# A matmul with a subtraction on one core: own semaphores, a PE loop over six m tiles, and shared weight loads

## The chip, the cores and the metric

The kernel runs on one core of a Trainium2 chip. The metric is the device time of one execution in microseconds; lower is better. The engines are named as the profile names them: PE is TensorE's matmul, PEld its weight loads, DVE is VectorE, ACT is ScalarE, SP issues the transfers. All 16 DMA engines of the core serve it.

## The reference

```python
batch, m, k, n = 16, 512, 1024, 768
def reference(x, weight, sub_value):          # all float32
    return (np.matmul(x, weight) - sub_value).astype(np.float32)
```

With the batch flattened there are 64 m tiles of 128 rows. 61.9 MB are read from memory and 25.2 MB written.

## The kernel before

For each m tile, ACT casts x to f16, the cast tile is transposed, PE multiplies it with the f16 weights that stay on chip (16 matmuls of 384 columns), and DVE subtracts. Most tiles are transposed by PE (four transposes of 32-bit words, put between the matmuls of the tile two before) and copied out by ACT. Fourteen tiles, in seven pairs at 18, 24, ... 54, are transposed by DVE instead, in sixteen instructions for each pair. The parts that matter here:

```python
LEAD_DVE = 7                 # a pair's casts are issued seven tiles ahead
PER = 4                      # DVE transposes issued behind one subtraction
ON_DVE = frozenset(range(18, 60, 6))
...
x16p_pool = ctx.enter_context(tc.tile_pool(name="x16p_pool", bufs=2))   # a pair, cast
xtp_pool = ctx.enter_context(tc.tile_pool(name="xtp_pool", bufs=2))     # a pair, transposed
psum_o_pool = ctx.enter_context(tc.tile_pool(name="psum_o", bufs=3, space=bass.MemoryType.PSUM))
...
def matmuls(mi, c):          # each matmul loads its own weights
    ...
    for r in range(2):
        for h in range(2):
            keep(nc.tensor.matmul(po_t[mi][:, h, :NS], xt_t[mi][:, 2*P*c + r : 2*P*(c+1) : 2],
                                  w_sb[:, c, r, h*NS : (h+1)*NS], ...))
...
for mi in range(HEAD, n_mt):
    t = mi + TA              # TA = 2
    tr = transposes(t) if t < n_mt and t - t % 2 not in ON_DVE else []
    for c in range(n_c):
        matmuls(mi, c)
        if tr:
            tr[c]()          # the fourth is followed by ACT's copy
    for t in range(mi, n_mt):
        if t - lead(t) == mi:    # LEAD_DVE for a pair's tiles, 4 for others
            cast(t)
    finish(mi)               # DVE: subtract, then the transfer out if a group is done
    if mi + LEAD_DVE - 1 in ON_DVE:
        waiting += transposes_dve(mi + LEAD_DVE - 1)
    for f in waiting[:PER]:
        f()
    del waiting[:PER]
```

A framework puts in the semaphores and hands out the buffers; everything is written out in a straight line.

## Time and profile before

| | before |
|---|---|
| time, median of 3 | 211.0 us (210.91 to 211.28) |
| span in the profile | 209.4 us |
| DMA engines busy | 97.7%, mean 417 GB/s |
| granted clock of PE, mean (1 is full speed) | 0.998 |

A share of busy time does not say who waits for whom. The views to read are the stretches (busy time of each engine in a given piece of the span) and the timeline. "T" below means the moment at which one tile's matmuls end and the next tile's begin. The lines are in the prediction.

### The profile page before, as it was taken

How to read it: one execution, taken by the hardware profiler on the slowest of the kernel's cores; microseconds unless marked ns; L12 is line 12 of the kernel's file. 1: busy time of each engine (PE TensorE's matmuls, PEld its weight loads, DVE VectorE, ACT ScalarE, POOL GpSimd, SP SyncE). 2: the span in 40 equal slices, each digit the busy share in tenths (PEclk: the TensorE clock that was granted, in tenths of full speed). 3: DMA queues.
4: the chain of work that ended last, by engine and by line, in shares of the span. 5: the costliest groups of instructions: out<-in, count | busy, mean ns of one | idle time of the engine just before them, and what ended most of it. 6: DMA issues, size and time to landing. Idle time of an engine off the chain costs nothing.

```text
span 209.4 us, 2967 instructions
## 1 busy us (share of the span) xinstructions
PE 198.4 (95%) x1249; PEld 130.4 (62%) x1249; DVE 114.1 (54%) x186; ACT 112.6 (54%) x115; POOL 0.7 (0%) x6
## 2 busy tenths in 40 slices
PE   7998789999979999999999999999999999999990
PEld 2464467676656576676666666667666766766660
DVE  0342044206149849929946965992994795332231
ACT  3555565675396183655727629355573760765410
POOL 1000000000000000000000000000000000000000
PEclk9999999999999999999999999999999999999999
DMA  6999999999999999999999999999999999999994
GB/s 221 420 426 424 424 438 439 433 443 426 391 455 415 442 427 423 454 413 432 435 421 449 423 413 444 451 418 421 418 441 440 423 437 418 426 446 427 415 383 167
DMA packets 5629, 87.22 MB, mean 417 GB/s; under 512 B 624, under 2 KB 624, under 8 KB 2032
## 3 DMA queue, kind: packets, MB, share of 16 engines
q1 hardware_dynamic: 5616, 87.03, 97.7%
q8 instruction: 10, 0.16, 0.3%
q14 instruction: 3, 0.02, 0.0%
HBM read 61.87 MB, written 25.17 MB: 416 GB/s over the span
## 4 chain that ended last, share of the span: by engine, by line
PE 68%; DMA 20%; ACT 4%; DVE 3%; SPq 1%; issue 1%
PE psum_o L177 60%; DMA x_ring<-in_x_dram 20%; PE psum_t L144 8%; ACT x_tile L135 2%; DVE xtp_tile L165 2%; ACT xt_tile L151 1%; DVE so_ring L189 1%; SPq L110 1%; SPq L122 1%; ACT x16p_tile L132 0%
## 5 line engine op out<-in xcount | busy, mean ns | idle before, releaser
L177 PE MATMUL psum_o<-w_sb,xt_tile 128*128 128x384 f16 x800 | 145.7, 326 | 1.7 <-ACT xt_tile L151 1.1
L177 PEld LDWEIGHTS <-xt_tile 128*128 128x128 f16 x800 | 78.2, 98 | 41.5 <-ACT xt_tile L151 1.9
L189 DVE TENSOR_TENSOR so_ring<-psum_o,so_ring 128x768 f32<-128x768 f32 x64 | 60.7, 957 | 61.2 <-PE psum_o L177 41.1
L151 ACT COPY xt_tile<-psum_t 128x1024 f16<-128x1024 f16 x50 | 50.6, 1012 | 75.7 <-PE psum_t L144 74.9
L165 DVE STREAM_TRANSPOSE xtp_tile<-x16p_tile 32x256 f32<-32x256 f32 x112 | 48.8, 436 | 18.9 <-ACT x16p_tile L132 17.2
L144 PE MATMUL psum_t<-ident,x_tile 128*128 128x128 f32 x200 | 52.5, 275 | 2.8 <-ACT x_tile L135 2.4
L135 ACT CAST x_tile<-x_ring 128x1024 f16<-128x1024 f32 x50 | 51.6, 1049 | 5.5 <-DMA x_ring<-in_x_dram 5.5
L177 PE MATMUL psum_o<-w_sb,xtp_tile 128*128 128x384 f16 x224 | 42.9, 326 | 0.3 <-DVE xtp_tile L165 0.3
L144 PEld LDWEIGHTS psum_t<-ident,x_tile 128*128 128x128 f32 x200 | 27.8, 142 | 16.8 <-ACT x_tile L135 4.7
L177 PEld LDWEIGHTS <-xtp_tile 128*128 128x128 f16 x224 | 21.8, 98 | 10.4 <-DVE xtp_tile L165 0.7
L132 ACT CAST x16p_tile<-x_ring 128x1024 f16<-128x1024 f32 x14 | 14.6, 1046 | 5.8 <-DMA x_ring<-in_x_dram 4.7
L205 PE MATMUL psum_o<-idle_x,idle_w 128*128 128x512 f16 x25 | 8.8, 508 | 1.3 <-DVE idle_x L200 1.3
L112 DVE CAST w_sb<-so_ring 128x768 f16<-128x768 f32 x8 | 4.1, 556 | 10.5 <-DMA so_ring<-in_weight_dram 10.5
L205 PEld LDWEIGHTS <-idle_w 128*128 128x128 f16 x25 | 3.0, 120 | 5.0 <-issue 3.2
L135 ACT ACT_TABLE_LOAD x1 | 1.3, 1283 | 0.7 <-PEq L277 0.7
L199 DVE MEMSET idle_w<- 128x64 uint32 x1 | 0.1, 112 | 0.8 <-PEq L277 0.8
masks.py:199 POOL TENSOR_SCALAR_AFFINE_SELECT ident<-ident 128x128 f32<-128x128 f32 x1 | 0.3, 292 | 0.1
L200 DVE MEMSET idle_x<- 128x256 uint32 x1 | 0.3, 272 | 0.0
masks.py:197 POOL MEMSET ident<- 128x128 f32 x1 | 0.2, 205 | 0.3 <-POOLq L277 0.3
L277 POOL MEMSET const-bfloat16-1.0<- 128x1 bf16 x1 | 0.1, 101 | 0.0
L277 POOL MEMSET const-uint8-127<- 128x1 uint8 x1 | 0.1, 101 | 0.0
L277 POOL MEMSET const-float32-0.0<- 128x1 f32 x1 | 0.1, 98 | 0.2 <-issue 0.2
(1 smaller groups left out, 0.1 us busy)
## 6 DMA issues: line engine op xcount, KB each, us to landing
so_ring<-in_sub_value_dram SPq DMA_DIRECT2D x7, 3072.0 KB, 24.2
out_dram<-so_ring SPq DMA_DIRECT2D x7, 3072.0 KB, 31.2
x_ring<-in_x_dram SPq DMA_DIRECT2D x5, 4096.0 KB, 22.3
x_ring<-in_x_dram SPq DMA_DIRECT2D x2, 2560.0 KB, 23.3
x_ring<-in_x_dram SPq DMA_DIRECT2D x3, 1536.0 KB, 19.8
so_ring<-in_weight_dram SPq DMA_DIRECT2D x4, 768.0 KB, 8.7
x_ring<-in_x_dram SPq DMA_DIRECT2D x3, 512.0 KB, 6.2
so_ring<-in_sub_value_dram SPq DMA_DIRECT2D x1, 1536.0 KB, 22.2
```

Source lines behind the costliest of these rows:

```text
L110: keep(nc.sync.dma_start(out=st, in_=w_c[at]))
L112: keep(nc.vector.tensor_copy(out=w_sb[:, at, r], in_=st[:, r]))
L122: keep(nc.sync.dma_start(out=here, in_=there))
L132: keep(nc.scalar.copy(out=x16_t["pair", first][:, mi - first], in_=x_in))
L135: keep(nc.scalar.copy(out=x16_t[mi], in_=x_in))
L144: keep(nc.tensor.transpose(ps_t[mi].bitcast(F32)[:, c * P : (c + 1) * P], x16_t[mi].bitcast(F32)[:, c * P : (c + 1) * P], ident,))
L151: keep(nc.scalar.copy(out=xt_t[mi], in_=ps_t.pop(mi)))
L165: keep(nc.vector.transpose(xt[b * Q : (b + 1) * Q, :, a * Q : (a + 1) * Q], x16[a * Q : (a + 1) * Q, :, b * Q : (b + 1) * Q],))
L177: keep(nc.tensor.matmul(po_t[mi][:, h, :NS], xt_t[mi][:, 2 * P * c + r : 2 * P * (c + 1) : 2], w_sb[:, c, r, h * NS : (h + 1) * NS], start ...
L189: keep(nc.vector.tensor_tensor(out=o, in0=po_t.pop(mi)[:, :, :NS], in1=o, op=mybir.AluOpType.subtract))
L205: keep(nc.tensor.matmul(idle_o[:, 0], idle_w, idle_x, start=True, stop=True))
L277: nc = _bacc.Bacc("TRN2", target_bir_lowering=False, num_devices=1)
```

## The change

The intent is a short PE program: six m tiles as the body of a loop that runs seven times. Waits in the loop compare semaphores with registers that only grow, so the kernel makes its own semaphores in one critical section and names its own buffers. Two matmuls that use the same stationary operand share one load. What goes with it, because the body of six tiles must name the same buffers each time: one output buffer for a DVE pair, a shorter lead, and six transposes at a time. The core of the diff:

```diff
+N16, NXT, NPT, NPO = 4, 4, 2, 3
+N16P, NXTP = 2, 1
-LEAD_DVE = 7
-PER = 4
+LEAD_DVE = 5
+PER = 6
+LOOP = (15, 6, 7)
...
+        with self.engine.Fori(0, len(bodies)):
+            self.emit(first, value=lambda sem, v: regs[sem.name], after=after)   # after: reg_add
...
         for r in range(2):
+            weights = xt[:, 2 * P * c + r : 2 * P * (c + 1) : 2]
+            pe.add(lambda weights=weights: nc.tensor.ldweights(weights, tile_position=(0, 0)), ...)
             for h in range(2):
-                keep(nc.tensor.matmul(
+                pe.add(lambda r=r, h=h, weights=weights: loaded_matmul(
...
+        first, size, times = LOOP
+        pe.emit(pe.ops[: marks[first]])
+        pe.emit_loop([pe.ops[a:b] for a, b in zip(ends, ends[1:])])
+        pe.emit(pe.ops[ends[-1] :])
```

More of the change, by code (lines that the diff above doesn't have):

```diff
@@ L31, with __init__, add, emit @@
 ]
+class Queue:
+    def __init__(self, nc, engine):
+        self.nc, self.engine, self.ops, self.seen = nc, engine, [], {}
+    def add(self, make, waits=(), then=None, always=False):
+        need = []
+        for sem, value in waits:
+            if value > 0 and (always or self.seen.get(sem.name, 0) < value):
+                self.seen[sem.name] = value
+                need.append((sem, value))
+        self.ops.append((make, need, then))
+    def emit(self, ops, value=lambda sem, v: v, after=lambda sem: None):
+        for make, need, then in ops:
+            for sem, v in need[:-1]:
+                self.engine.wait_ge(sem, value(sem, v))
+                after(sem)
+            ins = make()
+            if need:
+                sem, v = need[-1]
+                ins.wait_op(sem, value(sem, v), "sem-ge")
+                after(sem)
+            if then:
+                ins.then_inc(*then)
+    def emit_loop(self, bodies):
+        first, second = bodies[0], bodies[1]
+        sems, firsts, steps = {}, {}, {}
+        for one in bodies:
+            assert [[s.name for s, _ in n] for _, n, _ in one] == [[s.name for s, _ in n] for _, n, _ in first]
+        for make, need, then in first:
+            for sem, v in need:
+                sems[sem.name] = sem
+                firsts.setdefault(sem.name, []).append(v)
+        later = {}
+        for make, need, then in second:
+            for sem, v in need:
+                later.setdefault(sem.name, []).append(v)
+        grow = {s: later[s][0] - firsts[s][0] for s in firsts}
+        for n, one in enumerate(bodies):
+            at = {s: iter(v) for s, v in firsts.items()}
+            for _, need, _ in one:
+                for sem, v in need:
+                    assert v == next(at[sem.name]) + n * grow[sem.name]
+        for s, v in firsts.items():
+            steps[s] = [b - a for a, b in zip(v, v[1:] + [v[0] + grow[s]])]
+        regs = {s: self.engine.alloc_register(f"at_{s}") for s in sems}
+        for s, r in regs.items():
+            self.engine.reg_mov(r, firsts[s][0])
+        left = {s: iter(v) for s, v in steps.items()}
+        def after(sem):
+            step = next(left[sem.name])
+            if step:
+                self.engine.reg_add(regs[sem.name], regs[sem.name], step)
+        with self.engine.Fori(0, len(bodies)):
+            self.emit(first, value=lambda sem, v: regs[sem.name], after=after)
@@ L43 @@
     nc = tc.nc
-    keep = tc.keep_in_program_order
     x_flat = x.flatten_outer_dims()
@@ L60 @@
     w_c = weight.rearrange("(c p r) n -> c p r n", p=P, r=2)
-    def rows(view, mi, n):
-        return view[mi // S][:, mi % S : mi % S + n]
-    const_pool = ctx.enter_context(tc.tile_pool(name="const", bufs=1))
-    w_pool = ctx.enter_context(tc.tile_pool(name="w_pool", bufs=1))
-    x_pool = ctx.enter_context(tc.tile_pool(name="x_pool", bufs=1))
-    x16_pool = ctx.enter_context(tc.tile_pool(name="x16_pool", bufs=CA + 2))
-    xt_pool = ctx.enter_context(tc.tile_pool(name="xt_pool", bufs=TA + 3))
@@ L70 @@
-    x16p_pool = ctx.enter_context(tc.tile_pool(name="x16p_pool", bufs=2))
-    xtp_pool = ctx.enter_context(tc.tile_pool(name="xtp_pool", bufs=2))
-    so_pool = ctx.enter_context(tc.tile_pool(name="so_pool", bufs=1))
-    psum_t_pool = ctx.enter_context(tc.tile_pool(name="psum_t", bufs=2, space=bass.MemoryType.PSUM))
-    psum_o_pool = ctx.enter_context(tc.tile_pool(name="psum_o", bufs=3, space=bass.MemoryType.PSUM))
-    ident = const_pool.tile([P, P], F32)
-    make_identity(nc, ident)
-    w_sb = w_pool.tile([P, n_c, 2, N], F16)
@@ L82, with sbuf, psum @@
-    x_ring = x_pool.tile([P, NX, K], F32)
-    so_ring = so_pool.tile([P, NSO, N], F32)
-    x16_t, xt_t, ps_t, po_t = {}, {}, {}, {}
+    ctx.enter_context(tc.tile_critical(no_gpsimd_drain=True))
+    def sbuf(name, shape, dtype):
+        return ctx.enter_context(nc.sbuf_tensor(name, shape, dtype)).ap()
+    def psum(name, shape, dtype):
+        return ctx.enter_context(nc.psum_tensor(name, shape, dtype)).ap()
+    ident = sbuf("ident", [P, P], F32)
+    w_sb = sbuf("w_sb", [P, n_c, 2, N], F16)
@@ new lines @@
+    x_ring = sbuf("x_ring", [P, NX, K], F32)
+    so_ring = sbuf("so_ring", [P, NSO, N], F32)
+    x16_b = sbuf("x16_b", [P, N16, K], F16)
+    xt_b = sbuf("xt_b", [P, NXT, K], F16)
+    x16p_b = sbuf("x16p_b", [P, N16P, 2, K], F16)
+    xtp_b = sbuf("xtp_b", [P, NXTP, 2, K], F16)
+    idle_w = sbuf("idle_w", [P, P], F16)
+    idle_x = sbuf("idle_x", [P, 512], F16)
+    pt_b = psum("pt_b", [P, NPT, K], F16)
+    po_b = psum("po_b", [P, NPO, 2, 512], F32)
+    counter = {}
+    for name in ("ident", "idle", "w", "cast", "evac", "pair", "turn", "mul", "finish"):
+        counter[name] = tc.alloc_semaphore(name)
@@ new lines, with count @@
+    so_far = dict.fromkeys(counter, 0)
+    def count(name):
+        so_far[name] += 1
+        return (counter[name], 1)
+    sp, pe = Queue(nc, nc.sync), Queue(nc, nc.tensor)
+    act, dve, pool = Queue(nc, nc.scalar), Queue(nc, nc.vector), Queue(nc, nc.gpsimd)
+    pool.add(lambda: nc.gpsimd.memset(ident, 0.0), then=count("ident"))
+    pool.add(lambda: nc.gpsimd.affine_select(
+        out=ident, in_=ident, compare_op=mybir.AluOpType.not_equal, fill=1.0, base=0,
+        pattern=[[-1, P]], channel_multiplier=1,
+    ), waits=[(counter["ident"], 1)], then=count("ident"))
@@ new lines, with loaded_matmul @@
+    ready = (counter["pair"], counter["evac"])
+    def loaded_matmul(out, weights, moving, start, stop):
+        with nc.discard():
+            full = nc.tensor.matmul(out, weights, moving, start=start, stop=stop).ins
+        return nc.tensor.add_instruction(mybir.InstMatmult(
+            name=nc.get_next_instruction_name(), engine=full.engine, ins=list(full.ins), outs=list(full.outs),
+            start_tensor_calc=full.start_tensor_calc, stop_tensor_calc=full.stop_tensor_calc,
+            tile_size=full.tile_size, tile_position=full.tile_position, ldweights=False,
+        ))
@@ L88, with take @@
+    landed = {}
+    cast_at, evac_at, pair_at, turn_at, mul_at, finish_at, w_at = {}, {}, {}, {}, {}, {}, {}
+    slot = {}
+    used = dict.fromkeys(("x16", "xt", "x16p", "xtp", "pt", "po"), 0)
+    holder = {}
+    def take(pool_name, n, mi):
+        b = used[pool_name] % n
+        used[pool_name] += 1
+        slot[pool_name, mi] = b
+        before = holder.get((pool_name, b))
+        holder[pool_name, b] = mi
+        return b, before
     todo = list(TRANSFERS)
     done = {"w": set(), "x": set(), "s": set(), "o": set(), "cast": set(), "finish": set()}
+    staged = {}
@@ L105, in issue @@
             done[kind] |= span
+            sem = tc.alloc_semaphore(f"{kind}{at}")
             if kind == "w":
@@ L109, in issue @@
                 st = so_ring[:, first : first + 2]
-                keep(nc.sync.dma_start(out=st, in_=w_c[at]))
+                sp.add(lambda st=st, at=at: nc.sync.dma_start(out=st, in_=w_c[at]), then=(sem, 16))
                 for r in range(2):
-                    keep(nc.vector.tensor_copy(out=w_sb[:, at, r], in_=st[:, r]))
+                    dve.add(
+                        lambda at=at, r=r, st=st: nc.vector.tensor_copy(out=w_sb[:, at, r], in_=st[:, r]),
+                        waits=[(sem, 16)], then=count("w"),
+                    )
+                    staged[first + r] = so_far["w"]
+                w_at[at] = so_far["w"]
                 continue
@@ L118, in issue @@
             there = view[at // S][:, at % S : at % S + n]
-            if kind == "o":
-                keep(nc.sync.dma_start(out=there, in_=here))
-            else:
-                keep(nc.sync.dma_start(out=here, in_=there))
+            waits = []
+            if kind == "x" and need:
+                waits.append((counter["cast"], max(cast_at[t] for t in need)))
+            if kind == "s":
+                for t in need:
+                    waits.append((landed["o", t], 16))
+                for t in span:
+                    if t % NSO in staged:
+                        waits.append((counter["w"], staged.pop(t % NSO)))
+            if kind == "o":
+                waits.append((counter["finish"], max(finish_at[t] for t in need)))
+            for t in span:
+                landed[kind, t] = sem
+            if kind == "o":
+                here, there = there, here
+            sp.add(lambda here=here, there=there: nc.sync.dma_start(out=here, in_=there), waits, (sem, 16))
     def cast(mi):
@@ L128, in cast @@
         first = mi - mi % 2
+        waits = [(landed["x", mi], 16)]
         if first in ON_DVE:
             if mi == first:
-                x16_t["pair", mi] = x16p_pool.tile([P, 2, K], F16, name="x16p_tile")
-            keep(nc.scalar.copy(out=x16_t["pair", first][:, mi - first], in_=x_in))
-        else:
-            x16_t[mi] = x16_pool.tile([P, K], F16, name="x16_tile")
-            keep(nc.scalar.copy(out=x16_t[mi], in_=x_in))
+                b, before = take("x16p", N16P, mi)
+                if before is not None:
+                    waits.append((counter["pair"], pair_at[before]))
+            to = x16p_b[:, slot["x16p", first], mi - first]
+        else:
+            b, before = take("x16", N16, mi)
+            if before is not None:
+                waits.append((counter["turn"], turn_at[before]))
+            to = x16_b[:, b]
+        act.add(lambda: nc.scalar.copy(out=to, in_=x_in), waits, count("cast"))
+        cast_at[mi] = so_far["cast"]
         issue()
@@ L141, in f @@
             def f():
+                waits = []
                 if c == 0:
-                    ps_t[mi] = psum_t_pool.tile([P, K], F16, name="psum_t")
-                keep(nc.tensor.transpose(
-                    ps_t[mi].bitcast(F32)[:, c * P : (c + 1) * P],
-                    x16_t[mi].bitcast(F32)[:, c * P : (c + 1) * P],
-                    ident,
-                ))
-                if c == n_c - 1:
-                    xt_t[mi] = xt_pool.tile([P, K], F16, name="xt_tile")
-                    keep(nc.scalar.copy(out=xt_t[mi], in_=ps_t.pop(mi)))
-                    x16_t.pop(mi)
+                    b, before = take("pt", NPT, mi)
+                    waits.append((counter["cast"], cast_at[mi]))
+                    if before is not None:
+                        waits.append((counter["evac"], evac_at[before]))
+                b = slot["pt", mi]
+                words = pt_b[:, b].bitcast(F32)[:, c * P : (c + 1) * P]
+                from_ = x16_b[:, slot["x16", mi]].bitcast(F32)[:, c * P : (c + 1) * P]
+                last = c == n_c - 1
+                pe.add(lambda: nc.tensor.transpose(words, from_, ident), waits, count("turn") if last else None)
+                if last:
+                    turn_at[mi] = so_far["turn"]
+                    d, before = take("xt", NXT, mi)
+                    waits = [(counter["turn"], turn_at[mi])]
+                    if before is not None:
+                        waits.append((counter["mul"], mul_at[before]))
+                    act.add(lambda: nc.scalar.copy(out=xt_b[:, d], in_=pt_b[:, b]), waits, count("evac"))
+                    evac_at[mi] = so_far["evac"]
             return f
@@ L156, in transposes_dve @@
     def transposes_dve(mi):
-        x16 = x16_t.pop(("pair", mi)).bitcast(F32).rearrange("p j (c q) -> p (j c) q", c=n_c)
-        xt_p = xtp_pool.tile([P, 2, K], F16, name="xtp_tile")
-        xt_t[mi], xt_t[mi + 1] = xt_p[:, 0], xt_p[:, 1]
-        xt = xt_p.bitcast(F32).rearrange("p j (c m) -> p (j c) m", c=n_c)
-        def one(a, b):
-            def f():
-                keep(nc.vector.transpose(
+        x16 = x16p_b[:, slot["x16p", mi]].bitcast(F32).rearrange("p j (c q) -> p (j c) q", c=n_c)
@@ new lines, in transposes_dve, with one @@
+        blocks = [(a, b) for a in range(P // Q) for b in range(P // Q)]
+        def one(n, a, b):
+            def f():
+                waits = []
+                if n == 0:
+                    d, before = take("xtp", NXTP, mi)
+                    waits.append((counter["cast"], cast_at[mi + 1]))
+                    if before is not None:
+                        waits.append((counter["mul"], mul_at[before + 1]))
+                xt = xtp_b[:, slot["xtp", mi]].bitcast(F32).rearrange("p j (c m) -> p (j c) m", c=n_c)
+                last = n == len(blocks) - 1
+                dve.add(lambda: nc.vector.transpose(
@@ L166, in f @@
                     xt[b * Q : (b + 1) * Q, :, a * Q : (a + 1) * Q],
                     x16[a * Q : (a + 1) * Q, :, b * Q : (b + 1) * Q],
-                ))
+                ), waits, count("pair") if last else None)
+                if last:
+                    pair_at[mi] = so_far["pair"]
             return f
-        return [one(a, b) for a in range(P // Q) for b in range(P // Q)]
+        return [one(n, a, b) for n, (a, b) in enumerate(blocks)]
     def matmuls(mi, c):
+        first = mi - mi % 2
@@ L173, in matmuls @@
+        on_dve = first in ON_DVE
+        waits = []
         if c == 0:
-            po_t[mi] = psum_o_pool.tile([P, 2, 512], F32, name="psum_o")
+            b, before = take("po", NPO, mi)
+            waits.append((counter["pair"], pair_at[first]) if on_dve else (counter["evac"], evac_at[mi]))
+            if before is not None:
+                waits.append((counter["finish"], finish_at[before]))
+        if mi <= HEAD:
+            waits.append((counter["w"], w_at[c]))
+        xt = xtp_b[:, slot["xtp", first], mi - first] if on_dve else xt_b[:, slot["xt", mi]]
@@ L175, in matmuls @@
+        po = po_b[:, slot["po", mi]]
         for r in range(2):
+            weights = xt[:, 2 * P * c + r : 2 * P * (c + 1) : 2]
+            pe.add(lambda weights=weights: nc.tensor.ldweights(weights, tile_position=(0, 0)), [w for w in waits if w[0] in ready])
+            waits = [w for w in waits if w[0] not in ready]
             for h in range(2):
-                keep(nc.tensor.matmul(
-                    po_t[mi][:, h, :NS],
-                    xt_t[mi][:, 2 * P * c + r : 2 * P * (c + 1) : 2],
+                last = c == n_c - 1 and r == 1 and h == 1
+                pe.add(lambda r=r, h=h, weights=weights: loaded_matmul(
+                    po[:, h, :NS],
+                    weights,
@@ L182, in matmuls @@
                     stop=(c == n_c - 1 and r == 1),
-                ))
+                ), waits, count("mul") if last else None)
+                waits = []
+        if c == n_c - 1:
+            mul_at[mi] = so_far["mul"]
     def finish(mi):
@@ L188, in finish @@
         o = so_ring[:, mi % NSO].rearrange("p (h n) -> p h n", h=2)
-        keep(nc.vector.tensor_tensor(
-            out=o, in0=po_t.pop(mi)[:, :, :NS], in1=o, op=mybir.AluOpType.subtract
-        ))
+        po = po_b[:, slot["po", mi]]
+        dve.add(lambda: nc.vector.tensor_tensor(
+            out=o, in0=po[:, :, :NS], in1=o, op=mybir.AluOpType.subtract
+        ), [(landed["s", mi], 16), (counter["mul"], mul_at[mi])], count("finish"))
+        finish_at[mi] = so_far["finish"]
         issue()
     issue()
-    idle_w = const_pool.tile([P, P], F16)
-    idle_x = const_pool.tile([P, 512], F16)
-    nc.vector.memset(idle_w, 0.0)
-    nc.vector.memset(idle_x, 0.0)
-    idle_o = psum_o_pool.tile([P, 2, 512], F32, name="psum_o")
+    starts = len(dve.ops)
+    dve.add(lambda: nc.vector.memset(idle_w, 0.0), then=count("idle"))
+    dve.add(lambda: nc.vector.memset(idle_x, 0.0), then=count("idle"))
+    dve.ops = dve.ops[starts:] + dve.ops[:starts]
     def idle(n):
         for _ in range(n):
-            keep(nc.tensor.matmul(idle_o[:, 0], idle_w, idle_x, start=True, stop=True))
+            pe.add(
+                lambda: nc.tensor.matmul(po_b[:, NPO - 1, 0], idle_w, idle_x, start=True, stop=True),
+                [(counter["idle"], 2)],
+            )
     def lead(mi):
@@ L215 @@
     cast(0)
+    pe.add(lambda: nc.tensor.matmul(po_b[:, NPO - 1, 0], idle_w, idle_x, start=True, stop=True), [(counter["ident"], 2)])
     transpose_tile(0)
@@ L245 @@
     waiting = []
+    marks = {}
     for mi in range(HEAD, n_mt):
+        marks[mi] = len(pe.ops)
+        if LOOP and mi >= LOOP[0] and (mi - LOOP[0]) % LOOP[1] == 0 and mi <= LOOP[0] + LOOP[1] * LOOP[2]:
+            pe.seen.clear()
         t = mi + TA
@@ L262 @@
     assert not todo
+    marks[n_mt] = len(pe.ops)
+    for q in (sp, act, dve, pool):
+        q.emit(q.ops)
+    for t in range(n_mt):
+        if t == 0 or landed["o", t] is not landed["o", t - 1]:
+            nc.sync.wait_ge(landed["o", t], 16)
+    if LOOP:
+        first, size, times = LOOP
+        pe.emit(pe.ops[: marks[first]])
+        ends = [marks[first + size * n] for n in range(times + 1)]
+        pe.emit_loop([pe.ops[a:b] for a, b in zip(ends, ends[1:])])
+        pe.emit(pe.ops[ends[-1] :])
+    else:
+        pe.emit(pe.ops)
 _INS = ['x', 'weight', 'sub_value']
```

## The prediction

> **What bounds the kernel now.** I read the page's parts 1 and 2 first, then a table by stretches, then the order of instructions in time. Part 1 and the groups give the load of each engine:
>
> ```profile
> PE 198.4 (95%) x1249; PEld 130.4 (62%) x1249; DVE 114.1 (54%) x186; ACT 112.6 (54%) x115; POOL 0.7 (0%) x6
> ...
> L177 PEld LDWEIGHTS <-xt_tile 128*128 128x128 f16 x800 | 78.2, 98 | 41.5 <-ACT xt_tile L151 1.9
> L189 DVE TENSOR_TENSOR so_ring<-psum_o,so_ring 128x768 f32<-128x768 f32 x64 | 60.7, 957 | 61.2 <-PE psum_o L177 41.1
> ...
> L165 DVE STREAM_TRANSPOSE xtp_tile<-x16p_tile 32x256 f32<-32x256 f32 x112 | 48.8, 436 | 18.9 <-ACT x16p_tile L132 17.2
> ```
>
> TensorE and the DMA engines (97.7% in part 3) both look like a bound. The stretches decide. The three below are each one period of six m tiles, of which two get their transposed x from VectorE. The columns are start:end, length, then busy us (count) of PE, weight loads, DVE, ACT, POOL, then clock, DMA share and GB/s.
>
> ```profile
> 122.75:140.10 17.35, 17.35 (x115) 11.64 (x113) 12.71 (x22) 10.16 (x11) 0.00 (x0) 1.00 1.00 427
> 140.10:157.45 17.35, 17.35 (x114) 11.65 (x113) 12.74 (x23) 9.89 (x11) 0.00 (x0) 1.00 1.01 434
> 157.45:174.80 17.35, 17.35 (x114) 11.65 (x113) 12.73 (x22) 8.78 (x9) 0.00 (x0) 1.00 1.00 430
> ```
>
> Each period is 17.35 us to the hundredth, with PE busy throughout. A period set by transfers would not repeat so exactly while the rate moves from 427 to 434 GB/s. The chain of waits agrees: from 70.70 us to the last matmul it holds practically nothing but PE. So from there the kernel runs at PE's own pace, with DMA just keeping up. The timeline shows what that pace is made of, and how close DVE and ACT follow (start, length, engine):
>
> ```profile
> 152.24 5.36 PE L177 MATMUL psum_o<-w_sb,xt_tile 128*128 128x384 f16 x32
> 152.50 1.01 ACT L151 COPY xt_tile<-psum_t 128x1024 f16<-128x1024 f16 x1 [2.08 <-PE psum_t L144]
> 153.41 1.99 ACT L135 CAST x_tile<-x_ring 128x1024 f16<-128x1024 f32 x2
> 153.67 0.96 DVE L189 TENSOR_TENSOR so_ring<-psum_o,so_ring 128x768 f32<-128x768 f32 x1
> ...
> 154.64 1.80 DVE L165 STREAM_TRANSPOSE xtp_tile<-x16p_tile 32x256 f32<-32x256 f32 x4
> ...
> 156.47 0.96 DVE L189 TENSOR_TENSOR so_ring<-psum_o,so_ring 128x768 f32<-128x768 f32 x1
> ...
> 157.44 0.81 PE L177 MATMUL psum_o<-w_sb,xtp_tile 128*128 128x384 f16 x4
> 157.65 0.96 DVE L189 TENSOR_TENSOR so_ring<-psum_o,so_ring 128x768 f32<-128x768 f32 x1 [0.22 <-PE psum_o L177]
> ```
>
> 32 matmuls (two tiles without transposes) start at 152.24 and the next tile at 157.44: 5.20 us, 162.5 ns each, 2.60 us a tile. The chain shows 0.11 us for a transpose between matmuls, so a tile with four takes 3.04. Four such and two without: 4 x 3.04 + 2 x 2.60 = 17.36, the period seen. In the same lines DVE ends the last four transposes of a pair at 156.44, and PE takes that pair up at 157.44: with sixteen transposes spread over the ends of four tiles, DVE is ready 1.0 us early. That slack is the number to watch.
>
> **What the Trainium skill says.** "TensorE: Matmul & The Clock Gate", section "Back-to-back issue gap", gives N/2.4 + 2.5 ns for warm matmuls: 162.5 ns at N = 384, which the trace matches. Its section "Step-by-step: what each phase is for" says that the next weight load runs while the current matmul does; the 98 ns loads inside a 162.5 ns pitch agree. "Runtime: NRT & Kernel Launch", section "Instruction fetch mechanics", says that sequential fetch is mostly hidden and that a taken branch to a page not held must fetch it first; no run of before has a loop, and its instruction queues carry 0.3% of DMA time. Of the clock, "TensorE: Matmul & The Clock Gate", section "What's actually happening", has the array clock halved after about 3.4 us idle; in before the granted clock is 1.00 until the end.
>
> **The change, part by part.** *Shared weight loads*: 1024 loads become 512, some 50 us of load time gone, all of it under matmuls that already issue at the pitch of their columns: 0 us. *Loop*: some 0.1 MB less instruction fetch of 87 MB, 0.1%: 0 us. Register additions, and seven branches, are on PE's sequencer[...]; I put them at 0 too (see rivals). *Own semaphores*: an entry into the critical section, within a few tenths of a us.
>
> *What the loop forces* is what counts. Its body must name the same buffers each time, and a body has one VectorE pair. So the pair's output buffer goes from two to one (NXTP 1), and the transposes of the next pair may only start once the last pair is multiplied. The lead falls from 7 tiles to 5, and PER goes from 4 to 6. The instruction order on DVE confirms what follows: after the subtraction of tile 20 come six transposes, subtraction 21, six, subtraction 22, four; then subtraction 23. Sixteen transposes must now fit between tile 20's end and tile 24's start.
>
> I work one period, with 0 as the start of tile 21 (end of tile 20), by durations from the rows above.
> - PE would want tile 24 after tiles 21, 22, 23: tile 21 does transposes, 22 and 23 do not: 3.04 + 2.60 + 2.60 = **8.24**.
> - ACT: the copy of tile 22's transposes starts 0.26 after the tile's end (152.24 to 152.50); the pair's second cast is issued behind it now, starts 0.91 later and takes 1.05: ready at 2.22. The trace shows 0.03 from a cast's end to DVE, so DVE starts at 2.25 (subtraction 20 is done by 0.20 + 0.96 = 1.16).
> - DVE: four transposes take 1.80 with a step of about 0.03 to the next kind; so six are 2.70 + 0.02; a subtraction 0.99 with its step (136.35 to 137.34). 2.25 + 2.72 = 4.97; subtraction 21 to 5.96; six to 8.68; subtraction 22 to 9.67; four (1.80) to 11.47; PE starts 0.05 later (as at 70.65 to 70.70): **11.52**.
> PE therefore idles 11.52 - 8.24 = **3.28 us** before each pair. The cycle closes: three tiles from the pair's start to the next "tile 20 end", 9.12, plus 11.52 makes a period of 20.64 against 17.35.
>
> The first of seven pairs (tile 18) is cheaper. In before ACT sat waiting for the transfer of x tiles 16 to 23 until 56.56, because the pair's early cast stood in front of tile 14's copy; PE idled 1.10 there and 0.34 at 70.70. With lead 5 that copy is in front: tile 14 starts at 57.31, not 58.57. By the same sums cast 19 is ready at 62.57, the transposes end at 62.60 + 9.22 = 71.82, and tile 18 starts at 71.87 against 70.70: +1.17. The other six cost 6 x 3.28 = 19.7. Sum **+20.9**; with a few tenths for entry, 211.0 + 21 = **232 us**.
>
> **Rivals.** (1) *The loads or the instruction stream were a hidden cost, and the kernel gets faster or stays.* For it: weight loads are 62% busy and TensorE is the bound. Against: the pitch is exactly that of the columns, with no gap to remove; at best the early idle of some 1.4 us comes back, 209.6 us. It also needs DVE's 16 x 0.45 + 2 x 0.99 = 9.2 us to fit in 8.24, which fails even if the cast were no trouble (then 1.16 + 9.2 = 10.4, a stall of about 2.2, and some 225 us). (2) *The back edge of the loop or the register waits hold up PE's sequencer.* The loop's edge lies between tiles 20 and 21, at the start of the very stretch in which PE has 3.28 us to spare; up to about 1.7 us would vanish in the wait for DVE (subtraction 21 must be able to start at 4.97, and tile 21 ends at 3.04 + 0.20). Only a longer stall shows: 3 us each would add some 8 us. (3) *The idle time lets the clock drop.* 3.28 us is just short of the skill's 3.4; if it trips, at most 3.4 us at half speed cost 1.7 us a period, ten in all: 242. (4) *DMA is the bound and hides the stalls.* It is at 430 GB/s while PE never waits for it; with longer periods it only gets slack. Not more than 1 us from shorter last transfers.
>
> **Range and chances.** 232 follows from the sum; the step I chose most freely is when the pair's second cast ends (up to 1 us earlier in each of six periods: 226) and rival 3, upwards. Range 226 to 239. Slower by over 2% is nearly certain, since the 9.2 us of DVE work alone do not fit: 0.95; within 2% 0.03; faster 0.02.
>
> **What would show it.** Right: in the periods after 72 us PE idles about 3.3 us once, before the first matmul on the VectorE pair, released by the transposes on DVE; period about 20.6 us; matmul pitch still 162.5 ns; weight loads 512 for the product and some 226 others, and their busy time down by about 50 us without effect; DMA share near 0.9. Wrong: PE gaps at the loop's edge instead, a granted clock under 1 in the middle, a pitch other than 162.5, or DVE's transposes starting within about 1.2 us of tile 20's end.

## The result, and the profile after

The changed kernel is correct and takes 239.62 us, the median of four runs: 238.21, 241.03, 235.07 and 242.32, with mean granted clocks of 0.966, 0.952, 0.980 and 0.945. The kernel before took 211.01 us in the same rounds. The ratio is 1.121 (95% interval 1.108 to 1.134). Executions over 1.5% slower than the fastest of the same kernel are left out of the means. Such ratios are not quite the ratio of the medians; this one stands for 236.6 us. Two of the four runs count as slow by a rule that looks at the distance to the fastest run; the experiments show what that spread is.

The page of the changed kernel: busy times by engine, and the transfer queue.

```profile
PE 204.8 (87%) x1250; PEld 82.0 (35%) x738; DVE 114.1 (48%) x186; ACT 112.8 (48%) x115; POOL 0.7 (0%) x6
...
q1 hardware_dynamic: 5616, 87.03, 87.9%
```

The weight loads fell from 1249 to 738 and from 130.4 to 82.0 us, and it did not help. DVE and ACT do what they did, in a longer span. PE's own busy time went up from 198.4 to 204.8 us, which the removal of work cannot do. Two periods of six tiles, in the stretches of the changed kernel (start:end, length, busy us and count of PE, PEld, DVE, ACT, POOL, then granted clock, DMA share, GB/s):

```profile
122.28:144.60 22.32, 19.18 (x115) 7.44 (x64) 12.72 (x22) 9.72 (x11) 0.00 (x0) 0.92 0.92 362
101.63:122.28 20.65, 17.51 (x115) 6.94 (x64) 12.72 (x22) 9.73 (x11) 0.00 (x0) 1.00 1.01 433
```

The same 22 DVE instructions and the same PE work take 20.65 us where the clock is full and 22.32 where it is not; before, it was 17.35. The timeline of the period with the fallen clock, up to its pair (start, length, engine). Its T, the end of tile 32, is 122.28; tiles 33, 34 and 35 lie between T and the pair, tiles 36 and 37. They are tiles 20 to 24 of the prediction's sum, two loops later:

```profile
123.44 1.05 ACT L271 CAST x16p_b<-x_ring 128x1024 f16<-128x1024 f32 x1
...
124.52 2.68 DVE L316 STREAM_TRANSPOSE xtp_b<-x16p_b 32x256 f32<-32x256 f32 x6 [1.20 <-ACT x16p_b L271]
...
127.21 0.96 DVE L360 TENSOR_TENSOR so_ring<-po_b,so_ring 128x768 f32<-128x768 f32 x1
128.20 2.68 DVE L316 STREAM_TRANSPOSE xtp_b<-x16p_b 32x256 f32<-32x256 f32 x6
...
130.90 0.96 DVE L360 TENSOR_TENSOR so_ring<-po_b,so_ring 128x768 f32<-128x768 f32 x1
131.89 1.80 DVE L316 STREAM_TRANSPOSE xtp_b<-x16p_b 32x256 f32<-32x256 f32 x4
...
133.81 0.81 PE L175 MATMUL po_b<-w_sb,xtp_b 128*128 128x384 f16 x4 [3.14 <-DVE xtp_b L316]
```

DVE starts the pair when the cast is done, works without a gap, and PE starts 0.12 us after its last transpose, having idled 3.14 us. The seven pairs start at 71.88, 92.52, 113.17, 133.81, 156.13, 178.12 and 200.44: steps of 20.64, 20.65, 20.64, then 22.32, 21.99, 22.32. Four us behind the start of the third and of the fourth pair:

```profile
113.10:117.10 4.00, 3.93 (x26) 1.77 (x16) 1.73 (x2) 0.64 (x1) 0.00 (x0) 1.00 1.00 434
133.80:137.80 4.00, 3.99 (x18) 1.53 (x11) 0.87 (x1) 0.00 (x0) 0.00 (x0) 0.65 1.16 492
```

With the clock at 0.65 PE begins 18 instructions where it begins 26 at full clock. After the fourth to seventh pair of this execution the clock fell, after the first three it did not, although the wait was equally long.

### The profile page after: what moved, and what is told of

The parts are those of the page before. It is cut to its first block, busy times and chain, and to the rows that moved or that the text cites. A ratio compares the mean times of both kernels' runs of the same rounds, so it can differ in the third digit from the quotient of the medians.

```text
span 236.4 us, 2580 instructions
## 1 busy us (share of the span) xinstructions
PE 204.8 (87%) x1250; PEld 82.0 (35%) x738; DVE 114.1 (48%) x186; ACT 112.8 (48%) x115; POOL 0.7 (0%) x6
## 3 DMA queue, kind: packets, MB, share of 16 engines
q1 hardware_dynamic: 5616, 87.03, 87.9%
## 4 chain that ended last, share of the span: by engine, by line
PE 40%; DVE 26%; DMA 17%; ACT 10%; issue 3%; SPq 1%; ACTq 0%
PE po_b L175 34%; DVE xtp_b L316 20%; DMA x_ring<-in_x_dram 17%; DVE so_ring L360 6%; PE pt_b L289 6%; ACT xt_b L296 5%; ACT x16p_b L271 3%; ACT x_b L271 2%; SPq L223 1%; SPq L252 1%; ACTq L56 0%; SPq L482 0%; SPq L129 0%
## 5 line engine op out<-in xcount | busy, mean ns | idle before, releaser
L175 PE MATMUL po_b<-w_sb,xt_b 128*128 128x384 f16 x800 | 145.7, 326 | 0.4 <-DVE w_sb L226 0.4
L360 DVE TENSOR_TENSOR so_ring<-po_b,so_ring 128x768 f32<-128x768 f32 x64 | 60.8, 957 | 96.7 <-PE po_b L175 79.1
L296 ACT COPY xt_b<-pt_b 128x1024 f16<-128x1024 f16 x50 | 50.6, 1012 | 106.1 <-PE pt_b L289 105.3
L175 PE MATMUL po_b<-w_sb,xtp_b 128*128 128x384 f16 x224 | 48.9, 356 | 22.0 <-DVE xtp_b L316 22.0
L340 PEld LDWEIGHTS <-xt_b 128*128 128x128 f16 x400 | 39.2, 98 | 57.2 <-issue 53.6
L289 PE MATMUL pt_b<-ident,x_b 128*128 128x128 f32 x200 | 53.4, 279 | 2.9 <-ACT x_b L271 2.8
L271 ACT CAST x_b<-x_ring 128x1024 f16<-128x1024 f32 x50 | 51.6, 1048 | 7.6 <-DMA x_ring<-in_x_dram 7.5
L316 DVE STREAM_TRANSPOSE xtp_b<-x16p_b 32x256 f32<-32x256 f32 x112 | 48.8, 436 | 10.1 <-ACT x16p_b L271 8.4
L289 PEld LDWEIGHTS pt_b<-ident,x_b 128*128 128x128 f32 x200 | 28.4, 145 | 48.6 <-issue 42.6
L271 ACT CAST x16p_b<-x_ring 128x1024 f16<-128x1024 f32 x14 | 14.7, 1048 | 0.0
```

Of the source, the lines that this page charges most:

```text
L175: return nc.tensor.add_instruction(mybir.InstMatmult(name=nc.get_next_instruction_name(), engine=full.engine, ins=list(full.ins), outs=lis ...
L271: act.add(lambda: nc.scalar.copy(out=to, in_=x_in), waits, count("cast"))
L289: pe.add(lambda: nc.tensor.transpose(words, from_, ident), waits, count("turn") if last else None)
L296: act.add(lambda: nc.scalar.copy(out=xt_b[:, d], in_=pt_b[:, b]), waits, count("evac"))
L316: dve.add(lambda: nc.vector.transpose(xt[b * Q : (b + 1) * Q, :, a * Q : (a + 1) * Q], x16[a * Q : (a + 1) * Q, :, b * Q : (b + 1) * Q],), ...
L340: pe.add(lambda weights=weights: nc.tensor.ldweights(weights, tile_position=(0, 0)), [w for w in waits if w[0] in ready])
```

## The experiments

The theory after the result: (a) PE waits for DVE before each pair, because of one output buffer, lead and the order of casts, and not because of the loop, the semaphores or the loads; (b) the rest of the loss is the clock, which falls in some of these waits or just behind them. Twelve kernels were run; all gave correct results. Up to four shared one chip and its runs of the kernel before, whose medians were 211.17 to 211.29 us.

**e1_fill: is the rest the clock?** Eight idle matmuls in front of each pair, into the bank that the pair takes next:

```diff
+        if FILL and c == 0 and on_dve and mi == first:       # FILL = 8
+            bank = po_b[:, slot["po", mi], 0]
+            for n in range(FILL):
+                pe.add(lambda: nc.tensor.matmul(bank, idle_w, idle_x, start=True, stop=True), ...)
```

> The changed kernel, with eight idle 512-column matmuls (about 1.7 us) put on PE in front of each VectorE pair, into the output bank that the pair's first tile takes next. Theory (the wait for VectorE is 3.28 us a period whatever PE does, and the rest of the loss is the clock, which falls because PE is idle for 3.1 us): the pair starts at the same moments as before the clock falls, period 20.64 us in all seven, granted clock about 1.00, time about 232 us, all runs within 1 us. Rival (the clock has nothing to do with idle time, or the extra time comes from the loop): time stays at 235 to 242 with a clock under 0.98, or grows by the added matmuls, 7 x 1.7 = 12 us.

Measured: 231.79 us (231.46 to 232.23), clock 1.00 in three runs and 0.997 in one. PE has 56 more matmuls and the kernel is 7.8 us faster than the changed one by medians. The third and fourth pair in its timeline:

```profile
112.91 0.81 PE L176 MATMUL po_b<-w_sb,xtp_b 128*128 128x384 f16 x4 [1.38 <-DVE xtp_b L317]
...
133.53 0.81 PE L176 MATMUL po_b<-w_sb,xtp_b 128*128 128x384 f16 x4 [1.39 <-DVE xtp_b L317]
```

They are 20.62 us apart, as all seven are within 0.01 us. So DVE sets the moment whatever PE does meanwhile, and what was above 232 us in the changed kernel was the clock. Part (b) is shown, and the spread of its runs with it.

**e2_unrolled: is it the loop?** `LOOP = None`: the PE program written out, all else as changed.

> The changed kernel with the PE program written out in place of the loop, buffers, leads and all other engines as they are. Theory (loop, registers and its branches cost nothing on the chip; one output buffer and a lead of five cost all): 235 to 242 us as the changed kernel, periods of 20.64 us where the clock is full. Rival (the loop's branch or its register waits cost): up to the whole difference, back to 211 us.

Measured: 236.45 us (232.94 to 237.98; clocks 0.991, 0.973, 0.973, 0.969; ratio 1.122, two of the four runs slow). Pairs in the profiled run, which had the clock fall once, at its last pair:

```profile
112.53 0.82 PE L175 MATMUL po_b<-w_sb,xtp_b 128*128 128x384 f16 x4 [3.06 <-DVE xtp_b L316]
...
133.12 0.83 PE L175 MATMUL po_b<-w_sb,xtp_b 128*128 128x384 f16 x4 [3.06 <-DVE xtp_b L316]
```

The wait is there without any loop. The step is 20.59 us, 0.05 less than with it: PE starts 0.06 us after DVE's last transpose (133.12 after 133.06) where it waits against a number, and 0.12 us after it in the loop (133.81 after 133.69), where it waits against a register. The register is the likely reason, but was not tested apart from the loop. That is 0.3 us in six periods and all that the loop can be charged with here.

**e3_unrolled_lead7: does the rest of the change cost?** As e2, with `NXTP = 2`, `LEAD_DVE = 7`, `PER = 4`.

> As e2_unrolled, but with two output buffers for the pairs, a lead of seven tiles and four transposes at a time, as the kernel before has them; own semaphores and shared weight loads remain. Theory: periods of 17.35 us again, 211 us within 1 us, although half of the weight loads are gone. Rival (own semaphores or shared loads carry some of the slowdown, or a gain that was hidden): clearly above 213 or below 209 us.

Measured: 211.7 us (211.4 to 212.61), ratio 1.003 (0.9997 to 1.007), span 209.4. Own semaphores and 512 loads fewer neither gain nor cost anything that these runs resolve.

**e4_before_lead5: that part alone.** The kernel before with `bufs=1` for the transposed pair, `LEAD_DVE = 5`, `PER = 6`.

> The kernel before, with one output buffer for the pairs, a lead of five and six transposes at a time: that part of the change alone, without loop, own semaphores and shared loads. Theory: PE idles about 3.2 us before each pair, periods 20.6 us, and with the clock falling in some of them 232 to 242 us. Rival: stays near 211 us.

Measured: 234.96 us (232.04 to 235.23), ratio 1.108, clocks 0.974 to 0.990.

```profile
114.32 0.82 PE L177 MATMUL psum_o<-w_sb,xtp_tile 128*128 128x384 f16 x4 [2.98 <-DVE xtp_tile L165]
...
134.82 0.83 PE L177 MATMUL psum_o<-w_sb,xtp_tile 128*128 128x384 f16 x4 [2.97 <-DVE xtp_tile L165]
```

Three constants in the old kernel make the wait (step 20.50 us) and the falls of the clock. With e2 and e3 this shows part (a): the slowdown belongs to these three, taken together. No run changes the buffer alone or the lead of the transposes alone, and the 0.09 us between this step and e2's was not followed up.

**e5_per8: do the sums on DVE hold?** The changed kernel with `PER = 8`, so that only one subtraction, not two, is between the pair's transposes.

> The changed kernel with eight transposes behind a subtraction instead of six: sixteen in two tiles, one subtraction fewer in front of the pair. Theory, by the same sums: DVE starts at 2.25, eight transposes to 5.87, subtraction to 6.86, eight to 10.48, PE starts at 10.53: it idles 2.29 us (2.15 by the shift that the changed kernel's 3.14 showed), period 19.65 us; first pair 0.16 us late; about 225 us, and with idle stretches this short the clock stays at 1.00. Rival (the wait is set by something other than the sum of DVE's instructions): period stays at 20.64.

Measured: 231.78 us (230.23 to 232.67), ratio 1.094: a miss of nearly 7 us. The timeline tells the two terms apart:

```profile
113.68 0.81 PE L175 MATMUL po_b<-w_sb,xtp_b 128*128 128x384 f16 x4 [2.14 <-DVE xtp_b L316]
...
133.34 1.44 PE L175 MATMUL po_b<-w_sb,xtp_b 128*128 128x384 f16 x4 [2.15 <-DVE xtp_b L316]
...
154.62 0.81 PE L175 MATMUL po_b<-w_sb,xtp_b 128*128 128x384 f16 x4 [2.15 <-DVE xtp_b L316]
```

The wait is 2.15 us and the step with a full clock 19.66, both as expected. But behind 133.34 the first four matmuls take 1.44 us, not 0.81, and the next step is 21.28: the clock fell, in four of seven waits (mean 0.966 to 0.973 in the four runs). The expectation that 2.15 us of idling is too short for that was wrong.

**e11_per8_fill: was that all of the miss?** e5 with four idle matmuls (0.87 us) in front of each pair.

> e5_per8 with four idle matmuls (0.87 us) in front of each pair. Theory (e5_per8 missed its 225 us only by the clock, which fell in four or five of its seven waits although PE idled only 2.15 us): all seven pairs 19.66 us apart, granted clock 1.00, 225 us. Rival (eight transposes in a row cost something else): stays near 231.8.

Measured: 225.16 us (225.0 to 225.28), clocks 0.995 to 0.999, ratio 1.066. Pairs are 19.62 to 19.63 us apart and PE's remaining idle time is 1.25 us. It was all of it.

**e6_cast_early: is the second cast on the path?** In the changed kernel, a pair's casts are issued six tiles ahead, the transposes still five.

```diff
 LEAD_DVE = 5
+LEAD_CAST = 6
     def lead(mi):
-        return LEAD_DVE if mi - mi % 2 in ON_DVE else TA + CA
+        return LEAD_CAST if mi - mi % 2 in ON_DVE else TA + CA
```

> The changed kernel with the pair's two casts given to ACT one tile earlier (lead six for the casts, five still for the transposes). Theory: DVE no longer waits for ACT, starts right behind subtraction 20 at about 1.19 instead of 2.25, and the wait of PE falls by 1.06 to some 2.1 to 2.2 us, period 19.6, about 225 us, clock 1.00. Rival (the second cast was not on the path): period stays at 20.64 and the time at 235 to 242.

Measured: 225.24 us (225.02 to 225.47), ratio 1.066.

```profile
111.09 0.81 PE L176 MATMUL po_b<-w_sb,xtp_b 128*128 128x384 f16 x4 [1.85 <-DVE xtp_b L317]
...
130.44 0.81 PE L176 MATMUL po_b<-w_sb,xtp_b 128*128 128x384 f16 x4 [1.84 <-DVE xtp_b L317]
```

The step is 19.35 us, so the cast was worth 1.29 us a period, a little more than the 1.06 expected: the subtraction in front starts 0.09 us behind T here, not 0.20, and the transposes overlap its end by 0.09. The first pair waited 2.17 us and the clock fell behind it (0.72 in the 6 us from 70.0); behind the six waits of 1.84 to 1.85 us it stayed at 1.00.

**e7_loop12: what does a loop's edge cost where nothing hides it?** `LOOP = (15, 12, 3)`: a body of twelve tiles holds two pairs, so that two output buffers, lead seven and four at a time are possible.

> A loop again, but over twelve m tiles, three times, so that its body holds two pairs and two output buffers, lead seven, four transposes at a time. Nothing hides what a loop's edge costs here, as PE has no slack. Theory (the edge is free): 17.35 us periods and 211 to 212 us, like e3_unrolled_lead7. Rival (a branch or a fetch stalls PE where it was hidden by the wait for DVE): a gap of PE at each of two or three edges, 1 to 3 us each, 213 to 220 us.

Measured: 211.35 us (211.17 to 211.65), ratio 1.0004 (0.998 to 1.003).

```profile
100.00:117.35 17.35, 17.35 (x114) 6.95 (x64) 12.72 (x22) 9.72 (x10) 0.00 (x0) 1.00 1.01 437
117.35:134.70 17.35, 17.35 (x114) 6.95 (x64) 12.71 (x22) 9.82 (x10) 0.00 (x0) 1.00 1.01 434
```

PE is busy throughout. The edge in front of tile 39 lies in the second of these stretches, near 132.0. The edge in front of tile 27 lies between pairs 24 and 36, which start at 88.23 and 122.92, two periods of 17.35 apart. The loop as such shows no cost at these edges, and brings nothing: the instruction queue moved 0.08 MB instead of 0.16, of 87 MB.

**e8_own_loads: are shared loads worth anything?** As e3, each matmul with its own load again.

> As e3_unrolled_lead7, with each matmul loading its own weights again, as in the kernel before. Theory (loads lie under the matmuls): some 512 loads of 98 ns more on the weight row, the same time within 0.5% of e3_unrolled_lead7. Rival: slower by up to 1 us or more.

Measured: 212.31 us (212.04 to 212.39), ratio 1.0044 (1.002 to 1.007), against e3's 1.0034 on another chip, with 1250 loads for 738. The two intervals overlap; at most a few tenths of a per cent.

**e9_before_shift and e10_loop12_shift: can both be beaten?** PE idles 1.10 us near 57 us in the kernel before, behind an early cast. The pairs were moved to 20, 26, ... 62: `ON_DVE = frozenset(range(20, 64, 6))`, in the kernel before and in e7 (loop from tile 16).

> The kernel before with its VectorE pairs two tiles later (first at tile 20 instead of 18) and one more at the end (tile 62): eight pairs. Theory (PE's own pace is the bound): the early cast that stood in front of tile 14's copy while its transfer was missing is gone, which gives back PE's idle 1.10 and 0.34 us near 57 and 70 us, and four transposes each for two more tiles are off PE, 8 x 0.11 = 0.88 us: 209 us, 1% faster. Rival (DMA, busy at 1.00 throughout, is just as much the bound): 210.5 to 211.5, PE merely waits elsewhere, for x or for the values to subtract.

> The loop over twelve tiles of e7_loop12 with the same shift of the pairs (loop from tile 16). Theory: as e9_before_shift, 209 us; the loop neither gives nor takes. Rival: a DMA bound, 210.5 to 211.5.

Measured: 214.52 us (ratio 1.016) and 214.7 us (1.017) where 209 was expected: slower, clear of noise, though by less than 2%. Two lines of e9, from who waited for whom and from the timeline:

```profile
ACT x16p_tile L132 <- DMA x_ring<-in_x_dram: 16.6, 2, 8.6
```

```profile
172.74 0.83 PE L177 MATMUL psum_o<-w_sb,xt_tile 128*128 128x384 f16 x4 [2.38 <-ACT xt_tile L151]
```

The pairs 32 and 56 now begin with the first tile of a transfer of eight. Their casts, seven tiles ahead, make ACT wait for data up to 8.6 us, and the copies for PE stand behind them in ACT's order. PE loses 1.70 and 2.38 us at tiles that are no pair. In three of e9's five runs and four of e10's the mean clock is 0.986 to 0.988, as in e10's profiled run (0.987), in which the clock fell once, behind such a wait of 2.38 us.

**e12_before_pairs: and without that?** The kernel before with pairs at 20, 24, 30, ... 60.

> The kernel before with eight pairs at tiles 20, 24, 30, 36, 42, 48, 54, 60: only the first is moved by two tiles, and one is added at 60, so that no pair's early cast falls in front of a transfer of eight tiles as in e9_before_shift (pairs 32 and 56). Theory (PE's pace sets the end): PE's idle 1.10 and 0.34 us near 57 and 70 us and four transposes each of two tiles (0.88 us) are saved, some 2 us: 209 us. Rival (transfers, busy at 1.00, arrive when they arrive): PE waits for x later on what it saved, 210.5 to 211.5.

Measured: 211.3 us (211.17 to 211.54), ratio 1.0007 (0.9994 to 1.002); the 2 us that were expected did not come. The last subtraction of the kernel before, then that of e12:

```profile
204.49 0.96 DVE L189 TENSOR_TENSOR so_ring<-psum_o,so_ring 128x768 f32<-128x768 f32 x1 [1.64 <-PE psum_o L177]
```

```profile
201.39 0.96 DVE L189 TENSOR_TENSOR so_ring<-psum_o,so_ring 128x768 f32<-128x768 f32 x1 [1.64 <-PE psum_o L177]
```

All compute ends 3.10 us earlier, and both spans are 209.4 us. So an earlier end of compute brought nothing here: the last transfers end when the transfers before them let them. The kernel before has two bounds that meet: PE's pace, and 87 MB through DMA engines that are busy at 1.00 in the middle of the span. No version tried beats the kernel before.

## Why the prediction was right or wrong

The direction and the wait for DVE were right. The size was 7.6 us short by medians (232 against 239.62), and the median lies 0.6 us above the range; by the ratio (236.6 us) it was 4.6 us short and in the range, as are two runs, 235.07 and 238.21. What is missing from the sum is the clock.

- **PE's pace as the bound of before.** Right, and incomplete. The transfers were described as just keeping up; e12 shows that they are an equal bound. For a change that slows PE this makes no difference. But the best case of rival 1, 209.6 us from idle time given back, rests on PE alone; e12 gave that time back, and 211.3 us came.
- **Shared loads, loop, semaphores at 0.** Right: e3 and e8 for loads and semaphores, e7 for the loop. The loop with its register waits costs 0.05 us a pair (e2), which was put at 0.
- **The sum on DVE.** Right, term by term to 0.07 us. From T at 122.28: transposes start at 2.24 (2.25 in the sum), second subtraction at 4.93 (4.97), third at 8.62 (8.68), PE at 11.53 (11.52). The period is 20.64 as worked out. That it agrees to 0.01 us is partly luck, since two small misses cancel: DVE was done at 11.41 and not 11.47, and PE took 0.12 us and not 0.05 to start. The profile calls 3.14 us of it idle, not 3.28, since it lets the matmul before end at 130.67, later than its successor could start (T + 8.24 = 130.52).
- **The first pair.** Right: 71.88 against 71.87.
- **Rival 3, the clock.** This is the step that failed. It was put at nothing in the sum, because "3.28 us is just short of the skill's 3.4", as if PE had to stand still for the whole of that time. The clock fell in four of the seven waits of the profiled run, and in e5 with 2.15 us of idling; what it takes is shown below. A granted clock under 1 in the middle was one of the prediction's own signs of being wrong. The size of one fall was right: 1.68 us where the period shows it fully (22.32 less 20.64), against 1.7. By (time - 231.8)/1.68 with e1's time, an estimate, the four runs of the changed kernel had about 3.8, 5.5, 1.9 and 6.3 falls. The rival's size for all six periods, 242, is what the slowest run shows (242.32); the range stopped at 239.
- **DMA gets slack.** Right: 87.9% busy after 97.7%, with DMA share 1.00 still in the early periods.

In which of the equal waits the clock falls can be read from the kept traces. Their record of the granted clock has the falls of this execution at 135.01, 155.49, 179.38 and 199.86 us. The steps between them are 6, 7 and 6 times 3.413 us, and each fall lasts 3.41 us at half clock. In e4 and e5, too, all falls of the execution lie whole multiples of 3.413 us apart, and in all fourteen traces the first grant of the full clock lies such a multiple before the falls. So the clock is set at the borders of pieces of 3.413 us, whatever the program does there. Four such pieces of the changed kernel, then two of e2 (columns as above: PE's busy time stands behind the length, the clock is the third figure from the end):

```profile
111.12:114.53 3.41, 1.36 (x9) 0.64 (x6) 2.80 (x6) 0.00 (x0) 0.00 (x0) 1.00 1.06 456
114.53:117.94 3.41, 3.41 (x25) 1.52 (x15) 0.96 (x1) 1.48 (x2) 0.00 (x0) 1.00 0.96 413
131.60:135.01 3.41, 1.20 (x8) 0.53 (x5) 2.97 (x6) 0.00 (x0) 0.00 (x0) 1.00 0.93 404
135.01:138.42 3.41, 3.41 (x14) 1.32 (x8) 0.00 (x0) 0.00 (x0) 0.00 (x0) 0.50 1.09 461
```

```profile
192.82:196.23 3.41, 1.36 (x9) 0.64 (x6) 2.87 (x6) 0.00 (x0) 0.00 (x0) 1.00 0.94 404
196.23:199.64 3.41, 3.41 (x14) 1.26 (x8) 0.08 (x1) 0.00 (x0) 0.00 (x0) 0.50 0.07 26
```

PE idles 2.05 us of the first piece and the clock stays; it idles 2.21 us of the third, and in the next the clock is half. With all fourteen traces cut into such pieces, from the first full clock to the last matmul of each, 14 pieces end in a fall, and PE idled 2.05 us or more in each of them (least: 2.05 in e2, 2.06 in e5, 2.07 in e4). In no piece that ends without a fall did it idle more than 2.05 us (most: 2.05 in the changed kernel, 2.03 in e4). So about 2.05 us of idling within one piece decides, to 0.01 us or so, since the ends of matmuls are modelled. A border can cut a wait of 3.14 us so that neither piece gets that much; a wait of 1.85 us alone can't reach it. Where the borders lie differs from trace to trace, so the program alone does not say how many falls a run will have.

## What to carry to other kernels

A loop on one engine fixes the buffers of the others: count how many buffers the body allows, then add up the instructions of the engine that has to refill the single one between last use and next use. That sum, from durations of the old trace, gave the period to 0.01 us here, with two misses of about 0.07 us that cancelled. Price a wait of PE at more than its length once it passes about 2 us, because the clock may fall behind it: a stretch of idle matmuls in an unavoidable wait took off 7.8 us here, and better is to take the wait away. And before speeding up an engine that is 100% busy, see whether the transfers would end any sooner.

## What the Trainium skill lacked or had wrong

- "TensorE: Matmul & The Clock Gate", section "What's actually happening", has the clock fall after an idle window of about 3.4 us. The traces show such windows, of 3.413 us, but PE need not idle through one: 2.05 us of it was enough (e2, e5, e4), and no page gives that share. It fell behind waits of 3.14 us (changed kernel, four of seven), 2.15 (e5, four of seven) and 2.17 (e6, once); never behind those of 1.84 to 1.85 (e6, six), 1.39 (e1, seven) or 1.25 (e11, seven) in the profiled runs.
- The same page, section "Back-to-back issue gap", says that N/2.4 + 2.5 ns counts too much for large N in a stream of loads and matmuls. In these traces the stream kept 162.5 ns at N = 384, exactly the formula, with own loads (before) and with shared ones (e3, e7).
- "Runtime: NRT & Kernel Launch", section "Instruction fetch mechanics", calls runtime control flow expensive, for branches to code that is not among the pages held. A PE loop of twelve tiles showed no gap at its edges (e7, 17.35 us periods, 211.35 against 211.29 us); whether its body is among those pages was not tested, so this limits the page's warning and does not refute it. No page has the cost of a wait against a register: about 0.05 us more at the wait that counts (after against e2).
